# Two-layer encoder trunk on one core: the first transfers paced in the order of need, the entry's instructions kept in program order

## The chip, the core and the metric

The kernel runs on one core of one Trainium2 chip. The metric is device time in microseconds (us) for one execution, the median of repeated runs; lower is better. The engines are TensorE (PE, matmuls and transposes), VectorE (DVE), ScalarE (ACT), GpSimd (POOL) and SyncE (SP, which issues most transfers); 16 DMA engines move the data. Each engine takes its own instructions in the order in which they are listed for it and waits on semaphores for the others.

## What is computed

The reference, cut to the part that the entry of the kernel bears on (the rest of a layer in words):

```python
for l in range(DEPTH):                       # DEPTH = 2
    u = rmsnorm(x, norm_mix[l])              # x: 256 x 2048, float32
    proj = u @ w_in[l]                       # 2048 x 8256
    c_q, c_kv, k_pe, q_na, k_na, v_na, gate_a, gate_b = jnp.split(proj, IN_SPLITS, axis=-1)
    ...
    x = x + merged @ w_out[l]
    h = rmsnorm(x, norm_mlp[l]) @ w_ff1[l]   # 2048 x 8192
    x = x + jnp.square(jax.nn.relu(h)) @ w_ff2[l]
return rmsnorm(x, norm_final)
```

Between the split and `merged` stand two attentions over the 256 tokens: a latent attention (c_q, c_kv, k_pe) and a neighbourhood attention (q_na, k_na, v_na), each with 8 heads, each followed by an output projection and a sigmoid gate.

## The kernel before

**Number format.** Every matrix product is made of float32 values that are split into a high part (rounded to the format in which PE takes them) and a low part (what is left). A product is high times high, high times low and low times high, summed in PSUM. So each weight piece is first cast on ACT (`hi`, line 206) and then subtracted on DVE (`lo`, line 207), and each activation piece becomes a `pair`: the high half written by ACT, the low half by DVE (`split`, lines 164 to 171).

**Which loops run over what.** x is 256 tokens by 2048 features and stays in SBUF as two tiles `xt` (128 tokens each). For the products the features must lie on the partitions. `turned` (line 495) transposes x for two blocks of 128 features at a time: four PE transposes (line 502) into one PSUM bank, then ACT scales by the norm's gain and writes the high halves, DVE the low halves. Feature blocks in `MIXED` (pairs 1, 2, 3, that is k = 2 to 7) are first copied to a float32 tile `wide` (line 508), because a later product needs sums of them; the others go from the bank straight to a pair. The row norm itself is a sum of squares on ACT (`RowNorm.add`, line 350), one instruction for 128 tokens by 512 features; its result is only needed when the first product is read out.

The first product is the neighbourhood attention's first 512 query columns. `gemm_b` (line 277) runs over 16 blocks of k, two at a time, which makes eight steps; I call them step 0 to 7 and the weight piece of a step w0 to w7. A piece is 256 x 512 float32, 512 KB; w0 comes in two halves of 256 KB, each cast by itself. In a step PE makes 8 high matmuls (two k by four banks, line 284, 512 columns: both halves of the activation pair against the high weights) and 8 low ones (line 289, 256 columns: the high activations against the low weights). `weights` (line 181) is the generator that loads and splits the pieces; for this first product alone it loads two blocks at a time rather than four, and calls `before(k0)`, which is `enter` (line 651): it issues the loads of x that are due, makes the transposes and evictions of that step, and after every second step the norm sums of 512 features. The five small tables (mask, cos, sin and two more) are loaded at the end of it, on SP.

**What sets the order.** The program is written in one order, but the framework's scheduler sets the order within each engine by its own simulated timeline; only the bias loads of the neighbourhood heads (line 600) are kept where the program has them. Raw weight pieces have 3 buffers: a piece's transfer is issued when the low half of the third piece before it is made. `hi` and `lo` have 4 buffers each, PSUM 8 banks: the product under way holds 4 of them.

Of the kernel before, what the change touches and what calls it, by code (L numbers as in the profile page):

```python
# [39 lines left out]
P = 128  # L40
S = 256
# [34 lines left out]
def trunk(ctx: ExitStack, tc: tile.TileContext, x, w_in, w_uq, w_ukv, rpb, w_o_mla, w_o_na,  # L76
# [41 lines left out]

    def tables():
        for sb, src in ((mask_sb, mask), (cos_sb, cos), (sin_sb, sin), (turn, turns), (half, halves)):  # L120
            nc.sync.dma_start(sb, src)

    xt = [const.tile([P, D], F32, name=f"xt{t}") for t in range(2)]

# [36 lines left out]
        return acts[k]  # L161


    def split(dst, src, scale=1.0):

        nc.scalar.activation(dst[:, :S], src, AF.Copy, scale=scale)
        if isinstance(scale, float) and scale == 1.0:
            nc.vector.tensor_tensor(dst[:, S:], src, dst[:, :S].bitcast(F32), op=ALU.subtract)
        else:
            nc.vector.scalar_tensor_tensor(dst[:, S:], src, scale, dst[:, :S].bitcast(F32),  # L170
                                           op0=ALU.mult, op1=ALU.subtract)

    def parts(src):

# [6 lines left out]
    def weights(w, nk, c0, n, before=None):  # L181


        step = 2 if before else 4
        for k0 in range(0, nk, 2):
            if before:
                before(k0)
            if k0 % step == 0:
                raw = raws.tile([P, 2048], F32, tag="raw", name="raw", bufs=RBUFS)
                raw = raw[:, :step * n].rearrange("p (k n) -> p k n", n=n)  # L190
                load = w[k0 * P:(k0 + step) * P, c0:c0 + n].rearrange("(k p) n -> p k n", p=P)
                size = 1 if before and k0 == 0 else step
                for i in range(0, step, size):
                    nc.sync.dma_start(raw[:, i:i + size], load[:, i:i + size])
                if strips:
                    his, los = (t.rearrange("p (k n) -> p k n", n=n) for t in parts(raw.rearrange("p k n -> p (k n)")))
            if strips:
                yield k0, his[:, k0 % 4:k0 % 4 + 2], los[:, k0 % 4:k0 % 4 + 2]
                continue
            hi = wpool.tile([P, 1024], F32R, tag="hi", name="hi", bufs=hbufs)  # L200
            lo = wpool.tile([P, 1024], F32R, tag="lo", name="lo", bufs=hbufs)
            hi, lo = (t[:, :2 * n].rearrange("p (k n) -> p k n", n=n) for t in (hi, lo))
            src = raw[:, k0 % step:k0 % step + 2]
            for i in range(0, 2, min(size, 2)):
                i = slice(i, i + min(size, 2))
                nc.scalar.copy(hi[:, i], src[:, i])  # L206
                nc.vector.tensor_tensor(lo[:, i], src[:, i], hi[:, i].bitcast(F32), op=ALU.subtract)  # L207
            yield k0, hi, lo

    def weights_twice(w, nk, c0, n):  # L210
# [66 lines left out]
    def gemm_b(w, c0, acts, evac, before=None, ahead=None):  # L277
# [3 lines left out]
        for k0, wh, wl in weights(w, nk, c0, 512, before):  # L281
            for k in range(2):
                for m in range(4):
                    nc.tensor.matmul(ps[m], wh[:, k, m * P:(m + 1) * P], have(acts, k0 + k), start=k0 + k == 0, stop=False)  # L284
                    if m % 2:
                        tick()
            for m in range(4):
                for k in range(2):
                    nc.tensor.matmul(ps[m][:, :S], wl[:, k, m * P:(m + 1) * P], have(acts, k0 + k)[:, :S],  # L289
                                     start=False, stop=k0 + k == nk - 1)  # L290
# [51 lines left out]
    class RowNorm:  # L342
# [4 lines left out]

        def add(self, t, c4):
            junk = keep.tile([P, 512], mybir.dt.bfloat16, tag="junk", name="junk", bufs=1)
            nc.scalar.activation(junk, xt[t][:, c4 * 512:(c4 + 1) * 512], AF.Square,  # L350
                                 accum_out=self.sums[:, t, c4:c4 + 1])

        def scale(self):
            v = keep.tile([P, 2], F32, tag="var", name="var", bufs=2)
# [140 lines left out]
    def turned(src, c4, dst, scale, sums, pairs):  # L495


        for c in range(0, 4, 2):
            tp = abank()
            for i in range(2):  # L500
                for t in range(2):
                    nc.tensor.transpose(tp[:, (2 * i + t) * P:(2 * i + t + 1) * P],  # L502
                                        src(t)[:, (c + i) * P:(c + i + 1) * P], ident)
            j = 2 * c4 + c // 2
            if j in pairs:
                f = wide()
                for i in range(2):
                    nc.scalar.activation(f[:, i * S:(i + 1) * S], tp[:, i * S:(i + 1) * S], AF.Copy,
                                         scale=scale(2 * j + i))
            for i in range(2):  # L510
                a = pair()
                if j in pairs:
                    split(a, f[:, i * S:(i + 1) * S])
                else:
                    split(a, tp[:, i * S:(i + 1) * S], scale(2 * j + i))
                dst[2 * j + i] = a
            if j in pairs:
                sums[j] = f
# [125 lines left out]
    norm = RowNorm()  # L644
    xg, xf4 = [None] * NC, [None] * (NC // 2)

    def load(c0, c1):
        for t in range(2):
            nc.sync.dma_start(xt[t][:, c0:c1], x[t * P:(t + 1) * P, c0:c1])

    def enter(k0):
        if k0 in (0, 2):
# [8 lines left out]
                norm.add(t, k0 // 4)  # L661
        if k0 == 12:
            tables()

    for l in range(DEPTH):
        half_a = ExitStack()
# [298 lines left out]
```

## Time and profile before

| | us |
|---|---|
| runs before, median of 3 | 2616.18 (2616.12 to 2617.15) |
| the profiled execution's own time | 2617.45 |
| its span in the trace | 2615.3 |
| PE busy in the span | 2589.6 (99%) |
| DVE busy | 2184.0 (84%) |
| ACT busy | 1483.1 (57%) |

A profile's line gives the line of the kernel, the engine, the operation, what it writes and reads, and how often; `bank<-pair,hi` is a matmul into a PSUM bank. In a timeline the first number is the start in us from the span's beginning, the second how long the run of equal instructions took. In the chain of waits a piece ends where the next one was released. The trace of one execution is used throughout; its span is 2.15 us shorter than that execution's time.

### The profile page before, as it was taken

What the parts mean: (1) busy time and instruction counts of PE and PEld (TensorE: products, weight loads), DVE (VectorE), ACT (ScalarE), POOL (GpSimd) and SP (SyncE); (2) the same over time, 40 slices, a digit from 0 to 9 for tenths busy, and PEclk for the clock granted to TensorE, in tenths of its full rate; (3) what the DMA queues carried; (4) which work ended last, traced back from release to release, by engine and by line L of the source; (5) the groups of instructions that cost most, each with busy time, mean ns of one, the idle gap of its engine ahead of it and who ended that gap; (6) DMA issues with size and microseconds to landing.
All of it is one profiled execution on the core that took longest, in us unless ns stands there. A gap on an engine that the chain in (4) does not pass through costs nothing.

```text
span 2615.3 us, 32301 instructions
## 1 busy us (share of the span) xinstructions
PE 2589.6 (99%) x12450; PEld 2173.8 (83%) x12450; DVE 2184.0 (84%) x2571; ACT 1483.1 (57%) x1738; POOL 95.7 (4%) x117
## 2 busy tenths in 40 slices
PE   8999999999999999999999999999999999999998
PEld 7888888888888888888888888888888888888886
DVE  6678789789988898988667787896999988988885
ACT  6555556556655655556555555564666556565563
POOL 1100000000000010000001000000000000100000
PEclk9999999999999999999999999999999999999999
DMA  7555555555566575675565555544556766856753
GB/s 244 183 162 187 198 193 162 162 191 193 199 207 222 193 238 194 207 238 185 177 194 178 166 186 193 195 160 161 193 178 210 235 197 194 248 194 208 234 193 129
DMA packets 175562, 508.96 MB, mean 195 GB/s; under 512 B 13744, under 2 KB 18736, under 8 KB 175408
## 3 DMA queue, kind: packets, MB, share of 16 engines
q1 hardware_dynamic: 166496, 490.08, 56.4%
q0 software_dynamic: 8768, 16.78, 3.3%
q8 instruction: 97, 1.59, 0.2%
q14 instruction: 57, 0.47, 0.1%
q10 hardware_dynamic: 144, 0.04, 0.0%
HBM read 492.18 MB, written 2.10 MB: 189 GB/s over the span
## 4 chain that ended last, share of the span: by engine, by line
PE 88%; issue 8%; DVE 2%; ACT 1%; DMA 0%; POOL 0%; SPq 0%; POOLq 0%; DVEq 0%; ACTq 0%
PE bank L434 59%; PE bank L249 8%; PE bank L284 7%; PE bank L253 4%; PE bank L289 3%; PE bank L228 2%; PE bank L404 1%; PE bank L229 1%; PE bank L257 1%; PE bank L259 1%; PE bank L258 1%; DVE lo L178 1%; PE bank L565 1%; PE bank L502 0%; ACT hi L177 0%
## 5 line engine op out<-in xcount | busy, mean ns | idle before, releaser
L434 PE MATMUL bank<-hi,pair 128*128 128x512 f32 x5124 | 1284.4, 390 | 4.1 <-ACT hi L177 3.9
L434 PEld LDWEIGHTS bank<-hi,pair 128*128 128x128 f32 x5124 | 957.8, 188 | 204.8 <-ACT hi L177 5.6
L178 DVE TENSOR_TENSOR lo<-raw,hi 128x2048 fp32r<-128x2048 f32 (+3 forms) x416 | 741.6, 1796 | 73.8 <-ACT hi L177 47.6
L177 ACT CAST hi<-raw 128x2048 fp32r<-128x2048 f32 (+3 forms) x416 | 622.9, 1517 | 307.0 <-PE bank L434 178.6
L434 PE MATMUL bank<-lo,pair 128*128 128x512 f32 x2562 | 697.4, 390 | 0.0
L434 PEld LDWEIGHTS bank<-lo,pair 128*128 128x128 f32 x2562 | 479.7, 188 | 99.3
L177 ACT CAST hi<-sums 128x2048 fp32r<-128x2048 f32 (+1 forms) x150 | 244.9, 1637 | 291.4 <-DVE sums L475 171.8
L207 DVE TENSOR_TENSOR lo<-raw,hi 128x1024 fp32r<-128x1024 f32 (+1 forms) x225 | 273.6, 1220 | 123.0 <-ACT hi L206 121.2
L178 DVE TENSOR_TENSOR lo<-sums,hi 128x2048 fp32r<-128x2048 f32 (+1 forms) x150 | 290.8, 1947 | 98.6 <-ACT hi L177 59.0
L206 ACT CAST hi<-raw 128x1024 fp32r<-128x1024 f32 (+1 forms) x225 | 231.2, 1032 | 228.2 <-PE bank L249 88.6
L249 PE MATMUL bank<-hi,pair 128*128 128x512 f32 x1024 | 261.0, 391 | 0.0
L249 PEld LDWEIGHTS bank<-hi,pair 128*128 128x128 f32 x1024 | 190.3, 188 | 38.2
L483 DVE TENSOR_TENSOR wide<-wide,bank 128x512 f32<-128x512 f32 x336 | 214.7, 678 | 6.5 <-PE bank L434 6.4
L284 PE MATMUL bank<-pair,hi 128*128 128x512 f32 x768 | 203.3, 398 | 3.8 <-DVE pair L170 2.4
L471 DVE TENSOR_TENSOR sums<-raw 128x1024 f32<-128x1024 f32 x126 | 153.6, 1219 | 9.4 <-DMA raw<-in_w_ff 5.2
L284 PEld LDWEIGHTS bank<-pair,hi 128*128 128x128 f32 x768 | 136.3, 190 | 27.3 <-DVE pair L170 2.8
L253 PE MATMUL bank<-lo,pair 128*128 128x512 f32 x512 | 141.6, 391 | 0.0
L289 PEld LDWEIGHTS bank<-pair,lo 128*128 128x128 f32 x768 | 107.2, 191 | 8.5
L253 PEld LDWEIGHTS bank<-lo,pair 128*128 128x128 f32 x512 | 95.6, 188 | 19.4
L289 PE MATMUL bank<-pair,lo 128*128 128x256 f32 x768 | 111.7, 283 | 0.0
L413 ACT CAST pair<-wide 128x512 fp32r<-128x512 f32 x110 | 68.2, 620 | 58.6 <-DVE wide L372 56.4
L475 DVE TENSOR_TENSOR sums<-raw,sums 128x512 f32<-128x512 f32 x126 | 86.5, 687 | 2.0
(131 smaller groups left out, 1720.7 us busy)
## 6 DMA issues: line engine op xcount, KB each, us to landing
raw<-in_w_ff SPq DMA_DIRECT2D x256, 1024.0 KB, 5.2
raw<-in_w_in SPq DMA_DIRECT2D x124, 1024.0 KB, 5.0
raw<-in_w_out SPq DMA_DIRECT2D x32, 1024.0 KB, 5.3
raw<-in_w_o_na SPq DMA_DIRECT2D x16, 1024.0 KB, 5.0
raw<-in_w_o_mla SPq DMA_DIRECT2D x16, 1024.0 KB, 5.0
xt<-wide POOLq DMA_DIRECT2D x48, 256.0 KB, 5.4
raw<-in_w_ukv SPq DMA_DIRECT2D x8, 1024.0 KB, 5.0
raw<-in_w_uq SPq DMA_DIRECT2D x8, 768.0 KB, 4.5
```

Of the source, the lines that this page charges most:

```text
L177: nc.scalar.copy(hi, src)
L178: nc.vector.tensor_tensor(lo, src, hi.bitcast(F32), op=ALU.subtract)
L206: nc.scalar.copy(hi[:, i], src[:, i])
L207: nc.vector.tensor_tensor(lo[:, i], src[:, i], hi[:, i].bitcast(F32), op=ALU.subtract)
L249: nc.tensor.matmul(ps[t], a, wh[:, k], start=k0 + k + i == 0, stop=False)
L253: nc.tensor.matmul(ps[t], sides(have(acts, k0 + k), t)[0], wl[:, k], start=False, stop=k0 + k == nk - 1)
L284: nc.tensor.matmul(ps[m], wh[:, k, m * P:(m + 1) * P], have(acts, k0 + k), start=k0 + k == 0, stop=False)
L289: nc.tensor.matmul(ps[m][:, :S], wl[:, k, m * P:(m + 1) * P], have(acts, k0 + k)[:, :S], start=False, stop=k0 + k == nk - 1)
L434: nc.tensor.matmul(b[i], x, y, start=count[i] == 1, stop=count[i] == total[i])
L471: nc.vector.tensor_tensor(ts[0].rearrange("p (a n) -> p a n", a=2), raw[:, :512].rearrange("p (a n) -> p a n", a=1).to_broadcast([P, 2, 512]),
L475: final = nc.vector.tensor_tensor(t4, raw[:, 1536:], t2, op=ALU.subtract)
L483: add = lambda o, a, c: nc.vector.tensor_tensor(o, a, c, op=ALU.add)
```

## The change

Three things are changed, all of them in the entry (the first product of layer 0).

1. *Pacing.* A new function `paced` takes each load of x and of w0 to w7. It goes back over the loads before it and adds up their sizes, in units of 256 KB; the load that stands beyond three units must have landed before the new one is issued. The loads, and the tables too, are kept in program order on SP.
2. *Program order.* `pin` keeps an instruction in program order while `entering[0]` is true, up to step 7's `enter`. It is put around the high and low halves of weights and pairs, the norm sums, the copies to `wide` and the transposes, so on PE, ACT and DVE.
3. *The program's order itself.* `before(k0)` used to stand ahead of each step's weights. Now it is called for step 0 there, and for each later step in `gemm_b`, between the high and the low matmuls of the step before. Each of the two feature blocks of a step gets a PSUM bank of its own in the entry.

```diff
@@ tables()
-            nc.sync.dma_start(sb, src)
+            tc.keep_in_program_order(nc.sync.dma_start(sb, src))
...
+    entering = [True]
+    def pin(ins):
+        return tc.keep_in_program_order(ins) if entering[0] else ins
@@ weights()
         for k0 in range(0, nk, 2):
-            if before:
+            if before and k0 == 0:
                 before(k0)
...
-                    nc.sync.dma_start(raw[:, i:i + size], load[:, i:i + size])
+                    dma = nc.sync.dma_start(raw[:, i:i + size], load[:, i:i + size])
+                    if before:
+                        paced(dma, size)
...
-                nc.scalar.copy(hi[:, i], src[:, i])
-                nc.vector.tensor_tensor(lo[:, i], src[:, i], hi[:, i].bitcast(F32), op=ALU.subtract)
+                pin(nc.scalar.copy(hi[:, i], src[:, i]))
+                pin(nc.vector.tensor_tensor(lo[:, i], src[:, i], hi[:, i].bitcast(F32), op=ALU.subtract))
@@ gemm_b(), between the high and the low matmuls
+            if before and k0 + 2 < nk:
+                before(k0 + 2)
@@ turned()
-            tp = abank()
+            tp = [abank(), abank()] if entering[0] else [abank()] * 2
+            tp = [tp[i][:, i * S:(i + 1) * S] for i in range(2)]
...
+    landing = []
+    def paced(dma, tiles):
+        under_way = 0
+        for name, size in reversed(landing):
+            if under_way >= 3:
+                tc.add_manual_dep(dma.ins, name, mybir.DependencyInfo(mybir.DependencyClass.Sync,
+                                                                      mybir.DependencyReason.DATA))
+                break
+            under_way += size
+        tc.keep_in_program_order(dma)
+        landing.append((dma.ins.name, tiles))
@@ load()
-            nc.sync.dma_start(xt[t][:, c0:c1], x[t * P:(t + 1) * P, c0:c1])
+            paced(nc.sync.dma_start(xt[t][:, c0:c1], x[t * P:(t + 1) * P, c0:c1]), (c1 - c0) / 512)
@@ enter()
+        if k0 == 14:
+            entering[0] = False
```

The split, the norm sum and the transposes get `pin` in the same way. With this the lines move: 206/207 (cast and low half of weights) become 214/215, 284/289 (high and low matmuls) become 292/299, 502 (transposes) becomes 513, 508 (copy to `wide`) becomes 518, 166, 168 and 170 (pairs) become 172, 174 and 176, 350 (norm sum) becomes 360, 304 (norm's row) becomes 314, and 649 and 194 (loads of x and of weights) become 673 and 200.

What it does to the order of the instructions shows at three places. First PE, around the second step. `bank<-pair,hi` is a high matmul, `bank<-pair,lo` a low one, `bank<-ident,xt` a transpose of x for a later step; in brackets stand the semaphores that a row waits for (DMAHW0 to 7 are landings of transfers, in turn). Before, from the second four high matmuls of step 0:

```order
L284 MATMUL bank<-pair,hi 128x512 [waits DVE_49]
L284 MATMUL bank<-pair,hi 128x512 x3
L289 MATMUL bank<-pair,lo 128x256 x8
L502 MATMUL bank<-ident,xt_87 128x128 [waits DMAHW0_49]
L502 MATMUL bank<-ident,xt_87 128x128
L502 MATMUL bank<-ident,xt_88 128x128 [waits DMAHW1_49]
L502 MATMUL bank<-ident,xt_87 128x128
L502 MATMUL bank<-ident,xt_88 128x128 x2
L502 MATMUL bank<-ident,xt_87 128x128
L502 MATMUL bank<-ident,xt_88 128x128
L502 MATMUL bank<-ident,xt_87 128x128 [waits DMAHW3_49,PE_49]
L502 MATMUL bank<-ident,xt_87 128x128 [waits PE_49,Activation_49]
```

After the change, from the high matmuls of step 1:

```order
L292 MATMUL bank<-pair,hi 128x512 [waits DVE_49,Activation_49]
L292 MATMUL bank<-pair,hi 128x512 x3
L292 MATMUL bank<-pair,hi 128x512 [waits DVE_49]
L292 MATMUL bank<-pair,hi 128x512 x3
L513 MATMUL bank<-ident,xt_87 128x128 [waits DMAHW0_49,PE_49]
L513 MATMUL bank<-ident,xt_88 128x128 [waits DMAHW1_49]
L513 MATMUL bank<-ident,xt_87 128x128 [waits PE_49]
L513 MATMUL bank<-ident,xt_88 128x128
L299 MATMUL bank<-pair,lo 128x256 [waits DVE_49]
L299 MATMUL bank<-pair,lo 128x256 x7
L292 MATMUL bank<-pair,hi 128x512 [waits DVE_49,Activation_49]
```

Before, the transposes of two later steps and the beginning of a third stood together, ahead of the high matmuls of step 1. Now each step's high matmuls are followed by the transposes of the next step and then by its low matmuls, and this pattern repeats to step 6.

Second ACT, in the same stretch. `hi<-raw` is the cast of a weight piece (160 and 198 are w1 and w2 before, 162 and 201 after), `junk,sums<-xt` a norm sum, `wide<-bank` and `pair<-wide` the two instructions of an eviction. Before:

```order
L206 CAST hi_160<-raw_158 128x1024
L350 ACTIVATE junk_234,sums_89<-xt0_87 128x512
L350 ACTIVATE junk_236,sums_89<-xt1_88 128x512
L508 ACTIVATE wide_145<-bank_140,g_sb_80 128x256 x2
L166 ACTIVATE pair_148<-wide_145 128x256
L206 CAST hi_198<-raw_196 128x1024
L166 ACTIVATE pair_151<-wide_145 128x256
L350 ACTIVATE junk_306,sums_89<-xt0_87 128x512
L350 ACTIVATE junk_308,sums_89<-xt1_88 128x512
L508 ACTIVATE wide_187<-bank_182,g_sb_80 128x256 x2
L206 CAST hi_240<-raw_238 128x1024
```

After:

```order
L518 ACTIVATE wide_139<-bank_133,g_sb_80 128x256
L518 ACTIVATE wide_139<-bank_134,g_sb_80 128x256
L172 ACTIVATE pair_142<-wide_139 128x256
L172 ACTIVATE pair_145<-wide_139 128x256
L360 ACTIVATE junk_148,sums_89<-xt0_87 128x512
L360 ACTIVATE junk_150,sums_89<-xt1_88 128x512
L214 CAST hi_162<-raw_160 128x1024
L518 ACTIVATE wide_182<-bank_176,g_sb_80 128x256
L518 ACTIVATE wide_182<-bank_177,g_sb_80 128x256
L172 ACTIVATE pair_185<-wide_182 128x256
L172 ACTIVATE pair_188<-wide_182 128x256
L214 CAST hi_201<-raw_199 128x1024
```

Before, w1's cast stood ahead of the evictions of step 1 (wide_145) and w2's in the middle of them; now each cast stands behind all evictions and norm sums of its own step. The one exception is the end: behind w6's cast stand w7's and the two of the next product's first piece, and only then the evictions and norm sums of step 7. DVE has the low halves in the same new order; the reduction of the norm sums (`var`) comes after those of step 7's pairs, and one more low half of the next product's weights stands between it and the diagonals for the norm's row.

Third SP, with the loads of x (`xt<-in_x`) and of weights (`raw<-in_w_in`). Before, from the second loads of x:

```order
L649 DMA xt_87<-in_x 128x256
L649 DMA xt_88<-in_x 128x256
L194 DMA raw<-in_w_in 128x2x512
L649 DMA xt_87<-in_x 128x512 [waits DMAHW0_49]
L649 DMA xt_88<-in_x 128x512 [waits DMAHW1_49]
L194 DMA raw<-in_w_in 128x2x512 [waits DMAHW2_49]
L649 DMA xt_87<-in_x 128x512 [waits DMAHW3_49]
L649 DMA xt_88<-in_x 128x512 [waits DMAHW4_49]
L194 DMA raw<-in_w_in 128x2x512 [waits DMAHW5_49,DVE_49]
```

After:

```order
L673 DMA xt_87<-in_x 128x256
L673 DMA xt_88<-in_x 128x256 [waits DMAHW1_49]
L200 DMA raw<-in_w_in 128x2x512 [waits DMAHW2_49]
L673 DMA xt_87<-in_x 128x512 [waits DMAHW4_49,DMAHW0_49]
L673 DMA xt_88<-in_x 128x512 [waits DMAHW6_49]
L200 DMA raw<-in_w_in 128x2x512
L673 DMA xt_87<-in_x 128x512 [waits DMAHW3_49,DMAHW0_49]
L673 DMA xt_88<-in_x 128x512 [waits DMAHW1_49]
L200 DMA raw<-in_w_in 128x2x512 [waits DMAHW5_49,DVE_49]
```

The order of these nine is the same; the waits are on other landings: the second load of x for the other 128 tokens now waits for the first load of all, w1 for the second one, and so on. Further down the last loads of x stand behind w3 and w4 instead of w3 alone, and the tables behind w5 instead of ahead of w4. The table of the activation functions, which ACT loads first, now carries the wait for the gains (`g_sb`), because the first activation after it is one that uses them. After the entry the engines' orders differ again only around the output projection and the first MLP product of layer 0.

More of the change, by code (lines that the diff above doesn't have):

```diff
@@ L161, in have @@
         return acts[k]
+    entering = [True]
+    def pin(ins):
+        return tc.keep_in_program_order(ins) if entering[0] else ins
     def split(dst, src, scale=1.0):
-        nc.scalar.activation(dst[:, :S], src, AF.Copy, scale=scale)
+        pin(nc.scalar.activation(dst[:, :S], src, AF.Copy, scale=scale))
         if isinstance(scale, float) and scale == 1.0:
-            nc.vector.tensor_tensor(dst[:, S:], src, dst[:, :S].bitcast(F32), op=ALU.subtract)
+            pin(nc.vector.tensor_tensor(dst[:, S:], src, dst[:, :S].bitcast(F32), op=ALU.subtract))
         else:
-            nc.vector.scalar_tensor_tensor(dst[:, S:], src, scale, dst[:, :S].bitcast(F32),
-                                           op0=ALU.mult, op1=ALU.subtract)
+            pin(nc.vector.scalar_tensor_tensor(dst[:, S:], src, scale, dst[:, :S].bitcast(F32),
+                                               op0=ALU.mult, op1=ALU.subtract))
     def parts(src):
@@ L349, in add @@
             junk = keep.tile([P, 512], mybir.dt.bfloat16, tag="junk", name="junk", bufs=1)
-            nc.scalar.activation(junk, xt[t][:, c4 * 512:(c4 + 1) * 512], AF.Square,
-                                 accum_out=self.sums[:, t, c4:c4 + 1])
+            pin(nc.scalar.activation(junk, xt[t][:, c4 * 512:(c4 + 1) * 512], AF.Square,
+                                     accum_out=self.sums[:, t, c4:c4 + 1]))
         def scale(self):
@@ L498, in turned @@
         for c in range(0, 4, 2):
-            tp = abank()
+            tp = [abank(), abank()] if entering[0] else [abank()] * 2
+            tp = [tp[i][:, i * S:(i + 1) * S] for i in range(2)]
             for i in range(2):
                 for t in range(2):
-                    nc.tensor.transpose(tp[:, (2 * i + t) * P:(2 * i + t + 1) * P],
-                                        src(t)[:, (c + i) * P:(c + i + 1) * P], ident)
+                    pin(nc.tensor.transpose(tp[i][:, t * P:(t + 1) * P], src(t)[:, (c + i) * P:(c + i + 1) * P], ident))
             j = 2 * c4 + c // 2
@@ L507, in turned @@
                 for i in range(2):
-                    nc.scalar.activation(f[:, i * S:(i + 1) * S], tp[:, i * S:(i + 1) * S], AF.Copy,
-                                         scale=scale(2 * j + i))
+                    pin(nc.scalar.activation(f[:, i * S:(i + 1) * S], tp[i], AF.Copy,
+                                             scale=scale(2 * j + i)))
             for i in range(2):
@@ L514, in turned @@
                 else:
-                    split(a, tp[:, i * S:(i + 1) * S], scale(2 * j + i))
+                    split(a, tp[i], scale(2 * j + i))
                 dst[2 * j + i] = a
```

## The prediction

> **What bounds the kernel now.** I read the page first, then the windows of the first 30 us, then the chain of waits there, and last the waits of TensorE over the whole span. The page says who sets the time:
>
> ```profile
> PE 2589.6 (99%) x12450; PEld 2173.8 (83%) x12450; DVE 2184.0 (84%) x2571; ACT 1483.1 (57%) x1738; POOL 95.7 (4%) x117
> ```
>
> TensorE (PE) is busy 99% of the span, so a change of the entry can only move the little time in which PE stands still there. The windows (PE busy, weight loads, DVE, ACT, POOL, clock, DMA share, GB/s) show where:
>
> ```profile
> 5.00:10.00 5.00, 2.87 (x9) 2.38 (x10) 2.17 (x4) 3.10 (x8) 0.00 (x0) 1.00 0.92 255
> 10.00:15.00 5.00, 4.01 (x23) 3.41 (x21) 1.24 (x2) 3.47 (x9) 0.00 (x0) 1.00 1.01 373
> 15.00:20.00 5.00, 4.57 (x28) 3.62 (x27) 2.70 (x4) 4.97 (x12) 0.00 (x0) 1.00 0.93 283
> 20.00:25.00 5.00, 4.23 (x26) 3.58 (x25) 4.29 (x13) 5.00 (x14) 2.25 (x3) 1.00 0.55 160
> 25.00:30.00 5.00, 5.00 (x32) 4.46 (x31) 4.73 (x7) 3.41 (x7) 2.26 (x3) 1.00 0.76 223
> ```
>
> Up to 10 us PE waits for data and up to 20 us ScalarE (ACT) is full (4.97 of 5 us); from 25 us on PE is. The chain of waits (start, us, what) says the same in order of time:
>
> ```profile
> 3.54 7.94 DMA raw<-in_w_in
> ...
> 20.89 1.19 PE bank L284 x4
> ...
> 24.07 0.33 PE bank L502 x3
> 24.40 1.84 PE bank L284 x8
> 26.25 0.95 PE bank L289 x8
> ...
> 29.99 0.44 PE bank L304 x4
> ...
> 38.78 0.95 PE bank L289 x8
> ```
>
> The second weight piece, w1, lands late (7.94 us from issue), ACT then has to catch up, and from 20.89 us all is PE. A step of the first product costs PE 1.84 us for its 8 high matmuls, 0.95 for its 8 low ones, and 4 transposes at 0.11. At 38.78 + 0.95 = 39.73 us PE has done all eight steps, and beside them four high matmuls of the second product (4 x 0.23 = 0.92) and the four matmuls of the norm's row (0.44). So the first product alone ends at 39.73 - 1.36 = **38.37 us**; that is the figure to compare with.
>
> **The change, part by part.** I build the entry after the change from durations of before, in the new order of each engine. The first stretch:
>
> ```profile
> 0.74 0.40 ACTq L112 DMA_DIRECT2D g_sb<-in_gains  x1
> 1.17 1.28 ACT L206 ACT_TABLE_LOAD   x1 [1.17 <-PEq L954]
> 3.37 1.39 PE L502 MATMUL bank<-ident,xt 128*128 128x128 f32 x4 [3.37 <-DMA xt<-in_x]
> 5.34 0.62 ACT L206 CAST hi<-raw 128x512 fp32r<-128x512 f32 x1 [2.88 <-DMA raw<-in_w_in]
> 7.13 2.07 PE L284 MATMUL bank<-pair,hi 128*128 128x512 f32 x4 [2.38 <-DVE pair L170]
> 9.01 1.05 PE L502 MATMUL bank<-ident,xt 128*128 128x128 f32 x4
> 9.71 2.05 PE L284 MATMUL bank<-pair,hi 128*128 128x512 f32 x4
> g_sb<-in_gains ACTq DMA_DIRECT2D x1, 40.0 KB, 2.7
> ```
>
> The first transposes end at 3.37 + 1.39 = 4.76 as before, since the two transfers they need are still issued first. The table load now waits for the gains (issued at 0.74, landing 2.7 later, 3.44) and ends at 4.72, just in time: hidden, and 1.28 us late if those landed later. The rest of the loop's durations:
>
> ```profile
> 16.11 0.62 ACT L350 ACTIVATE junk<-xt 128x512 bf16<-128x512 f32 x1
> 17.49 0.82 ACT L508 ACTIVATE wide<-bank,g_sb 128x256 f32<-128x256 f32 x2
> 18.20 1.04 ACT L206 CAST hi<-raw 128x1024 fp32r<-128x1024 f32 x1
> 19.27 1.23 DVE L207 TENSOR_TENSOR lo<-raw,hi 128x1024 fp32r<-128x1024 f32 x1 [1.79 <-ACT hi L206]
> 21.70 0.72 ACT L166 ACTIVATE pair<-wide 128x256 fp32r<-128x256 f32 x2
> 21.92 0.27 PE L502 MATMUL bank<-ident,xt 128*128 128x128 f32 x1
> 22.32 0.47 ACT L166 ACTIVATE pair<-bank,g_sb 128x256 fp32r<-128x256 f32 x1
> 22.83 0.48 DVE L170 SCALAR_TENSOR_TENSOR pair<-bank,g_sb,pair 128x256 fp32r<-128x256 f32 x1
> 23.22 0.16 DVE L362 TENSOR_SCALAR half<-col 128x2 f32<-128x2 f32 x1
> 23.29 0.67 DVE L300 TENSOR_SCALAR diag<-ident,col 128x128 f32<-128x128 f32 x2
> 24.56 0.85 ACT L166 ACTIVATE pair<-bank,g_sb 128x256 fp32r<-128x256 f32 x2
> 25.28 1.08 ACT L206 CAST hi<-raw 128x1024 fp32r<-128x1024 f32 x1
> ```
>
> Read from start to start on ACT: two norm sums 17.49 - 16.11 = 1.38, two copies to a wide tile 0.71, two pairs from it 22.32 - 21.70 = 0.62, two pairs straight from the bank 25.28 - 24.56 = 0.72, a cast 1.04 until its user may start (19.27, 0.03 after its end).
>
> *The pinned order makes a ring.* In the new order PE has the high matmuls of step i, then the transposes of step i+1, then the low matmuls of step i, then the high ones of i+1. ACT has the evictions of step i+1, its norm sums, then the cast of w(i+1). Both take their rows in order. So the high matmuls of i+1 wait for the cast, the cast stands behind the evictions, these wait for the transposes, and those stand behind the high matmuls of step i. Only the low matmuls lie outside the ring. Before, ACT could cast a weight piece while the transposes were still to come, so it worked on during the matmuls. The ring's length, from the first high matmul of one step to that of the next: 1.84 for the high ones, two transposes issued (0.11 apart) and the second's 0.27, about 0.1 to ACT (21.92 + 0.27 = 22.19 to 22.32): 2.3. Then ACT. With wide tile and norm 2.3 + 0.71 + 0.62 + 1.38 + 1.04 + 0.05 = 6.10; with wide tile alone 4.72; from the bank with norm 5.49; from the bank alone 4.11. PE's own work in it is 1.84 + 0.43 + 0.95 = 3.22, so it stands still 0.9 to 2.9 us in each.
>
> *Start.* ACT begins at 4.8: evictions to 5.52, cast of the first half of w0 to 6.14, PE starts at 6.2 (before: 7.13). Its 8 matmuls run slowly, as the first eight of before did (four from 7.13 to 9.01, 1.88): 3.76, to 9.96; the transposes at 0.70 for four (9.01 to 9.71): two are done at 10.6, four at 10.9. ACT: copies 10.7 to 11.36, pairs to 11.98, norm to 13.36, cast to 14.4. Step 1 starts at 14.45. Whether PE is still slow there is a bound: at full rate all of it comes 3.76 - 1.84 + 0.70 - 0.43 = 2.2 earlier.
>
> *Steps 2 to 6* follow with the rings of steps 2 (wide), 3 (wide, norm), 4 (bank), 5 (bank, norm), 6 (bank): 14.45 + 4.72 + 6.10 + 4.11 + 5.49 + 4.11 = 38.98.
>
> *Step 7.* Behind the cast of w6 ACT's list has three casts (w7 and both halves of the next product's first piece, n0) ahead of the evictions of step 7. n0 may be issued when the low half of w5 is made. Transfers, in the windows at 3.5, 4.9 and 26 us, and on the page (KB each, median us to landing):
>
> ```profile
> raw<-in_w_in SPq DMA_DIRECT2D x1, 512.0 KB, 7.9
> raw<-in_w_in SPq DMA_DIRECT2D x1, 512.0 KB, 9.0
> raw<-in_w_in SPq DMA_DIRECT2D x2, 1024.0 KB, 8.4
> raw<-in_w_in SPq DMA_DIRECT2D x124, 1024.0 KB, 5.0
> ```
>
> Step 5 starts at 34.87, its cast ended 0.05 earlier, the low half of w5 at 36.08, n0 lands 5.0 later at 41.1. Casts to 43.18, first pair 43.65, DVE 0.48 more: step 7 starts at 44.2 and ends at 44.2 + 2.79 = 46.99. Then PE has the first matmul of the norm's row, which now waits: pairs to 43.90, norm sums to 45.28, a cast to 46.32, its low half on DVE to 47.58 (the column's own arithmetic lies beside it), half and the first diagonal 0.07 + 0.34. PE goes on at **48.05 us**, with the same work done as at 38.37 before.
>
> *Pacing.* w1 lands at 11.4 at the latest if pacing does nothing, and is not cast before 13.36; w2, at worst 9.0 after an issue near 7, lands at 16 for a cast at 18.1. So the earlier landings buy nothing once the ring stands, and the new waits of SP cost nothing: behind the waiting transfers on SP stand only later ones, whose users are later still. The tables now go out after w5, at about 22 us; their user on POOL feeds DVE at 85 us:
>
> ```profile
> L612 DVE SCALAR_TENSOR_TENSOR s<-bank,mb x8: 411/414/423, 85.0 to 100.0; 128x256 f32<-128x256 f32 x8
> ```
>
> *The rest.* After the entry the order differs once more, at the output projection and the first MLP product of layer 0. The largest wait of PE after the entry is 3.9 us in the whole span (who waits, for whom: us in total, times, longest), and the stretch that runs over DVE at 613 us is entered from PE, so a late PE moves it along:
>
> ```profile
> PE bank L434 <- ACT hi L177: 3.9, 4, 1.1
> ...
> 598.94 14.58 PE bank L434 x64
> ```
>
> I take 0 for it, bounds -2 and +2 (half of the 3.9, either way).
>
> **Sum.** 48.05 - 38.37 = +9.7 us. The profiled execution took 2617.45 us around a span of 2615.3; the median of the three runs is 2616.18, 1.3 lower. The difference is added to the median: **2625.9 us**. Bounds: no slow clock -2.2, n0 and the norm's chain in time -2.1 (1.1 and 1.0), later order -2: 2619.6 with all three, 2621.6 with the first two; n1, the piece behind n0, landing in 8.4 instead of 5.0 +3.4, later order +2: 2631.3.
>
> [...] The rows at 7.13 and 9.71 show PE at half speed for its first dense 4 us, while the windows grant it 1.00. [...]
>
> **Rivals.** (a) *Half rate comes back.* The longest gap, 6.10 - 3.22 = 2.9 us ahead of step 3, puts PE back to the speed of 7.13 us. A ring then grows by 1.92 + 0.27 = 2.2; two rings pass before dense work (6.4 us a step at half speed) releases it: +4.4, 2630.3. For it: slow matmuls after 2.4 us of idle at 7.13. Against: those were the first, never warm. Chance 0.13. (b) *The other side: early data wins.* The first chain link (7.94 us of w1) goes and ACT runs far enough ahead that PE is never held after 6.2. Then 3.76 + 0.70, seven steps of high ones (7 x 1.84), eight of low ones (7.6) and seven of transposes (3.1) end it at 34.2, 4.2 earlier: 2612.0, or 2609.8 with a warm clock. It decides if a cast of w(i+1) can pass the evictions; ACT's 5.00 of 5 us speaks for room on ACT being the point, the fixed rows of ACT speak against. Chance 0.08. (c) *Given back.* All 3.9 us of the later wait for casts vanish, as these get ahead of a late PE: 2622.0. Chance 0.08; against it, that stretch is entered from PE. (d) *No effect:* the rows run in another order than listed, or the ring's waits and the earlier start cancel, 2616.2. Chance 0.05; the listed order of before is the one that its trace shows.
>
> **How the numbers follow.** The ring as summed has 0.66, its time is the forecast. A measurement of this kernel tells about 0.2%, 5.2 us, from no change. Slower: the ring, (a) and (c), 0.87. Within: (d) and 0.05 of (b), 0.10. Faster: 0.03, (b) with a warm clock. The range runs from 2621 (two favourable bounds, and (c)) to 2632 (both unfavourable ones, and (a) with 1.7 us more); it leaves out (b) and (d), 0.13, and a few hundredths where several bounds meet on one side.
>
> **What would show it.** In the windows of the changed kernel PE is busy near 3.2 of every 4 to 6 us from 15 to 45 us, and ACT idles while PE runs the high matmuls. In the waits, PE's high matmuls (line 292 now) wait for the cast at line 214, five or six times, 0.9 to 2.9 us each; DMA ends no wait after 7 us. The last low matmuls of step 7 end near 47. If PE is dense from 20 us, or its waits end on pairs or DMA, the ring is wrong; matmuls of 0.43 us after 15 us show (a).

## The result, and the profile after

The changed kernel takes 2630.59 us (median of 6 executions, 2626.24 to 2631.03), the kernel before 2616.34 beside it: +14.25 us. The ratio of the mean times, here and for all runs below, is 1.0050, with a 95% interval of 1.0037 to 1.0063. The forecast was +9.7 us, 2625.9. The profiled execution took 2630.78 around a span of 2628.8.

TensorE's (PE's) rows of the timeline (start, us, ..., count, and in brackets the idle time just before and what ended it), the high matmuls of the eight steps and the first of the norm's row:

```profile
6.17 3.78 PE L292 MATMUL bank<-pair,hi 128*128 128x512 f32 x8 [1.43 <-DVE pair L176]
...
14.21 3.51 PE L292 MATMUL bank<-pair,hi 128*128 128x512 f32 x8 [2.57 <-ACT hi L214]
...
20.41 2.11 PE L292 MATMUL bank<-pair,hi 128*128 128x512 f32 x8 [1.30 <-ACT hi L214]
...
26.57 3.02 PE L292 MATMUL bank<-pair,hi 128*128 128x512 f32 x8 [2.67 <-ACT hi L214]
...
31.94 2.11 PE L292 MATMUL bank<-pair,hi 128*128 128x512 f32 x8 [0.28 <-ACT hi L214]
...
37.50 3.59 PE L292 MATMUL bank<-pair,hi 128*128 128x512 f32 x8 [2.06 <-ACT hi L214]
...
43.27 2.12 PE L292 MATMUL bank<-pair,hi 128*128 128x512 f32 x8 [0.69 <-ACT hi L214]
...
48.33 2.12 PE L292 MATMUL bank<-pair,hi 128*128 128x512 f32 x8 [1.56 <-DVE pair L176]
...
52.52 0.46 PE L314 MATMUL bank<-diag,ones 128*128 128x128 f32 x2 [1.13 <-DVE diag L310]
```

In six steps the wait ends on the cast (`ACT hi L214`), as forecast. But eight high matmuls take 2.11 us in some steps and 3.02 to 3.59 in steps 1, 3 and 5, the ones behind waits of 2.06 us or more. The norm's row starts at 52.52, against 38.37 for the same work before: +14.15, the whole loss. What lies behind it takes 2628.8 - 52.52 = 2576.3 us, before 2615.3 - 38.37 = 2576.9.

The windows of the same execution (PE, PE's weight loads, DVE, ACT, POOL, granted clock, DMA share, GB/s) show the slow steps in the clock:

```profile
5.00:10.00 5.00, 3.83 (x10) 2.95 (x11) 2.16 (x4) 1.66 (x4) 0.00 (x0) 1.00 0.86 269
10.00:15.00 5.00, 2.43 (x14) 2.13 (x13) 1.57 (x3) 3.71 (x9) 0.00 (x0) 0.89 0.84 291
15.00:20.00 5.00, 4.11 (x20) 3.28 (x18) 1.18 (x3) 2.02 (x5) 0.00 (x0) 0.77 0.69 212
20.00:25.00 5.00, 3.50 (x20) 2.90 (x20) 1.99 (x3) 2.55 (x8) 0.00 (x0) 1.00 0.44 129
25.00:30.00 5.00, 3.43 (x11) 2.69 (x12) 1.23 (x1) 1.52 (x3) 0.00 (x0) 0.75 0.37 92
```

ACT, full from 15 to 20 us before (4.97 of 5), is busy for 1.52 to 2.55 of every 5 us from 15 to 30 us here, and DMA's share there falls from 0.69 to 0.37: no engine is the bound, each waits its turn. ACT's timeline shows the ring from the other side:

```profile
25.49 1.03 ACT L214 CAST hi<-raw 128x1024 fp32r<-128x1024 f32 x1
30.05 0.90 ACT L172 ACTIVATE pair<-bank,g_sb 128x256 fp32r<-128x256 f32 x2 [3.54 <-PE bank L513]
30.85 1.04 ACT L214 CAST hi<-raw 128x1024 fp32r<-128x1024 f32 x1
```

After the cast of one piece ACT stands still for 3.54 us until PE has made the transposes (L513), not for a transfer; it evicts them at 30.05 and casts the next piece at 30.85, and PE waits for that cast.

### The profile page after: what moved, and what is told of

It is laid out like the page before. It is cut to its first block, busy times and chain, and to the rows that moved or that the text cites. A ratio compares the mean times of both kernels' runs of the same rounds, so it can differ in the third digit from the quotient of the medians.

```text
span 2628.8 us, 32302 instructions
## 1 busy us (share of the span) xinstructions
PE 2594.6 (99%) x12450; PEld 2177.0 (83%) x12450; DVE 2185.9 (83%) x2571; ACT 1482.9 (56%) x1738; POOL 98.3 (4%) x117
## 4 chain that ended last, share of the span: by engine, by line
PE 88%; issue 8%; DVE 2%; ACT 1%; DMA 1%; POOL 0%; POOLq 0%; DVEq 0%; SPq 0%; ACTq 0%
PE bank L444 59%; PE bank L257 8%; PE bank L292 7%; PE bank L261 4%; PE bank L299 3%; PE bank L236 2%; PE bank L414 1%; PE bank L237 1%; PE bank L265 1%; PE bank L267 1%; PE bank L266 1%; DVE lo L184 1%; PE bank L575 1%; PE bank L513 0%; ACT hi L214 0%
## 5 line engine op out<-in xcount | busy, mean ns | idle before, releaser
L214 ACT CAST hi<-raw 128x1024 fp32r<-128x1024 f32 (+1 forms) x225 | 230.8, 1031 | 210.8 <-PE bank L257 82.2
```

The lines of the kernel that those rows point to most:

```text
L214: pin(nc.scalar.copy(hi[:, i], src[:, i]))
```

## The experiments

Theories. **Ring**: the fixed order closes a loop cast, high matmuls, transposes, evictions, cast, and its waits are all of the loss. **Ring and clock**: those waits also bring the half clock back (0.50 granted from 13.85 to 17.26, from 27.50 to 30.92 and from 37.74 to 41.16 us), which is the 4.4 us that the ring lacks. Rivals: **transfers** (the pacing, not the order, moves the time) and **place** (the loss is at the end of the entry). In all runs the reference's work is done in full; some add idle matmuls.

**1. No pacing, order kept.**

```diff
-            if under_way >= 3:
+            if under_way >= 3 and False:
```

> The changed kernel without the pacing waits: the loads go out in the same order as soon as a buffer is free, and the listed order of PE, ACT and DVE is the changed kernel's. Theory (the ring of cast, high matmuls, transposes and evictions costs the time): w1 lands by about 11.4 us at the latest, ahead of its cast at 13.1, so nothing changes: 2628 to 2632 us, and PE's high matmuls wait for ACT's casts as in the changed kernel. Rival (the waits of the pacing hold back data that PE and ACT need): at least half of the 14 us come back, 2616 to 2623.

Measured: 2629.24 us (2626.78 to 2631.81), ratio to before 1.0051 (1.0038 to 1.0063). The loss stays, so the pacing isn't its cause. Two rows of PE:

```profile
13.69 2.12 PE L292 MATMUL bank<-pair,hi 128*128 128x512 f32 x8 [2.67 <-ACT hi L214]
...
24.67 2.51 PE L292 MATMUL bank<-pair,hi 128*128 128x512 f32 x8 [2.67 <-ACT hi L214]
```

The same waits for casts. Here one wait of 2.67 us is followed by full speed. Behind the next, just as long, the matmuls begin at full speed too, and the granted clock falls to 0.50 only at 26.20 us, for 3.41 us; the step's eight low matmuls then take 2.06 instead of 1.20. In this trace the clock does not follow the length of a wait alone.

**2. Pacing alone, on the kernel before** (and the five tables keep their place on SP).

```diff
-            nc.sync.dma_start(xt[t][:, c0:c1], x[t * P:(t + 1) * P, c0:c1])
+            paced(nc.sync.dma_start(xt[t][:, c0:c1], x[t * P:(t + 1) * P, c0:c1]), (c1 - c0) / 512)
...
+                    if before:
+                        paced(dma, size)
```

> The kernel before with the pacing alone: the loads and the tables in program order with the pacing waits, no instruction of PE, ACT or DVE pinned, the transposes called ahead of each step's weights as before. Theory (ring): no ring, so no loss; w1 lands by 8 to 9 us instead of 11.48, which is worth 0 to 3 us: 2613 to 2617. Rival (pacing holds data back): 2624 to 2631.

Measured: 2617.36 (2615.79 to 2619.88), ratio 1.0005 (0.9996 to 1.0014): no difference that can be told, 0.4 above the expected range. PE's waits in its first 55 us:

```profile
PE bank L504 <- DMA xt<-in_x: 6.3, 4, 3.3
```

Beside the first 3.3 us, which the kernel before has too, PE waits another 3.0 us for x in three pieces, the longest 1.66. Step 1 starts earlier (14.11 rather than 15.47), and the later x takes that back.

**3. No fixed order, pacing kept.**

```diff
     def pin(ins):
-        return tc.keep_in_program_order(ins) if entering[0] else ins
+        return ins
```

> The changed kernel without the pins on PE, ACT and DVE (pacing, the moved call of the transposes and the two banks stay), so the scheduler sets these orders: it lists w1's cast ahead of step 1's evictions. Theory (ring): the ring is open, PE is dense from about 20 us on as before: 2612 to 2618. Rival (pacing, or the new place of the transposes, not the pinned order): 2626 to 2631.

Measured: 2619.78 (2617.68 to 2621.92), ratio 1.0013 (1.0005 to 1.0022). Of the loss of 14.25 us 4.0 are left, so some 10 go with the fixed order, but the time is 1.8 above the upper end I gave. The rows of PE, then of ACT, show where:

```profile
31.70 0.60 PE L314 MATMUL bank<-diag,ones 128*128 128x128 f32 x4
34.98 1.51 PE L292 MATMUL bank<-pair,hi 128*128 128x512 f32 x4 [2.67 <-DVE pair L176]
36.28 1.91 PE L299 MATMUL bank<-pair,lo 128*128 128x256 f32 x8
```

```profile
30.33 1.99 ACT L214 CAST hi<-raw 128x1024 fp32r<-128x1024 f32 x2 [2.93 <-DMA raw<-in_w_in]
32.23 1.20 ACT L172 ACTIVATE pair<-bank,g_sb 128x256 fp32r<-128x256 f32 x3
```

PE is dense from 20 to 31 us, then the second half of step 6 waits 2.67 us for its eviction. The scheduler put this and step 7's two evictions behind the next product's first casts, which themselves waited 2.93 us for their transfer; the granted clock is down after it (0.66 from 35 to 40 us, and 1.91 for eight low matmuls that take 1.11 to 1.20 elsewhere). So there is a second place, the end of the entry.

**4. The ring opened by one position.** The cast of the next weight piece stands ahead of the evictions of the next step, all else fixed as it was:

```diff
             if before and k0 + 2 < nk:
-                before(k0 + 2)
+                before.fetch(k0 + 2)
+                piece = next(pieces)
+                before(k0 + 2)
```

> The changed kernel with everything pinned and paced as it is, but each next weight piece is fetched and cast ahead of the evictions of its step, so ACT's list is cast of w(i+1), evictions of step i+1, norm sums. Theory (ring): the ring loses the cast (1.04) and the norm sums (1.38 in every second step); what is left, high matmuls, transposes, one copy or none, one pair and its low half, is 3.3 to 3.8 us a step against PE's own 3.2, with no gap over 1 us up to step 6, so the half clock does not come back: step 7 starts near 33 us instead of 48.3 and the time is 2612 to 2617. Rival (pinning as such, or pacing, costs the time): 2626 to 2631.

Measured: 2617.82 (2616.49 to 2621.5), ratio 1.0010 (1.0001 to 1.0019); 0.8 above the range. Of its timeline, steps 5 to 7 and the norm's row:

```profile
30.77 2.11 PE L296 MATMUL bank<-pair,hi 128*128 128x512 f32 x8 [0.30 <-DVE pair L176]
...
36.43 3.55 PE L296 MATMUL bank<-pair,hi 128*128 128x512 f32 x8 [2.16 <-DVE pair L176]
...
40.89 0.38 PE L321 MATMUL bank<-diag,ones 128*128 128x128 f32 x2
```

From step 1 to step 6 the steps start 3.4 to 4.0 us apart, near PE's own work, with waits of at most 0.53: one move, of the cast with its low half, opens the ring and takes 12.2 of the 14.25 us. The rest is step 7, whose evictions stand behind three casts and three low halves, and the half clock after 2.16 us of waiting (0.67 granted from 35 to 40 us; eight high matmuls in 3.55).

**5. The norm sums out of the ring** (behind the cast of their step instead of ahead of it; the end of the pinned stretch moves with the last of them):

```diff
         for k0, wh, wl in weights(w, nk, c0, 512, before):
+            if before:
+                before.sums(k0)
```

> The changed kernel with only the norm sums moved: they stand behind the cast of their step instead of ahead of it, so that they run on ACT while PE has the high matmuls. Theory (ring, with the half clock brought on by its gaps): the rings of steps 1, 3 and 5 shorten by 1.38 each, 4.1 in all, and with the gaps of 2.1 to 2.7 us cut to 0.7 to 1.3 the half clock stays away and another 0 to 4.4 come back: 2622 to 2627, the rings of steps 3 and 5 at 4.7 and 4.1 us. Rival (ACT's order does not matter, PE is held by something else): 2629 to 2632.

Measured: 2627.58 (2626.88 to 2628.25), 0.6 above the range. The two rings with sums shrink from 6.16 and 5.56 to 4.80 and 4.19, by about the 1.38 us of the sums, no wait in them exceeds 1.31 us, the clock stays at 1.00, and step 7 starts at 39.31, 9.0 earlier than in the changed kernel. Then:

```profile
39.31 2.14 PE L294 MATMUL bank<-pair,hi 128*128 128x512 f32 x8 [0.69 <-ACT hi L214]
...
47.32 0.77 PE L316 MATMUL bank<-diag,ones 128*128 128x128 f32 x2 [4.93 <-DVE diag L312]
...
47.74 3.76 PE L294 MATMUL bank<-pair,hi 128*128 128x512 f32 x8
```

The norm's diagonal is 4.93 us late, and the clock falls in that wait (0.57 granted from 45 to 50 us and 0.74 from 50 to 55; eight high matmuls in 3.76). The last norm sum now stands behind two of the next product's casts (it starts at 41.66), and on DVE two more low halves and three read-outs of the product stand between the reduction of the sums (43.13) and the diagonal (46.77). Most of the gain is given back at the next place in the same chain.

**6. The waits filled, to keep the clock up.** Idle matmuls of a 128x128 tile of ones behind the low halves of steps 0, 2 and 4:

```diff
+            if before and k0 in (0, 4, 8):
+                idle = abank()
+                for i in range(16):
+                    pin(nc.tensor.matmul(idle[:, :P], ones, ident, start=True, stop=True))
```

> The changed kernel with 16 matmuls of 128 columns, whose result is not used, behind the low matmuls of steps 0, 2 and 4, that is inside PE's three gaps of 2.1 to 2.7 us (16 x 0.11 = 1.8 us of work in each). Theory (the half clock is brought on by these gaps): the windows from 12 to 45 us show a granted clock of 1.00, the eight high matmuls of steps 1, 3 and 5 start to end take 2.1 us instead of 3.0 to 3.6, and the time falls by about 4 us to 2626 or 2627. Rival (the clock falls for another reason, or its cost is hidden): no change or slower by the work added, 2630 to 2634.

Measured: 2630.4 (2629.7 to 2632.44). The price was wrong: each of these matmuls shows as two instructions of PE, so 16 took

```profile
12.09 3.73 PE L304 MATMUL bank<-ident,ones 128*128 128x128 f32 x32
15.58 2.08 PE L292 MATMUL bank<-pair,hi 128*128 128x512 f32 x8
```

3.73 us instead of the 1.8 meant, and made the three rings 0.7 to 1.4 us longer. The eight high matmuls of steps 1, 3 and 5 did run at full speed (2.08 to 2.10 us, 1.00 granted up to 45 us). The test says that the clock stayed up behind the three filled waits, and nothing yet of what that is worth.

**7. The same with 8 instead of 16**, so that the filler ends inside the wait.

> As the changed kernel, with 8 idle 128x128 matmuls of ones (16 instructions of TensorE, 1.75 us by the 3.73 us that 32 took in the run with 16) behind the low halves of steps 0, 2 and 4, in the waits of 2.57, 2.67 and 2.06 us after which the changed kernel ran at half clock. Nothing of the reference's work is left out. If the half clock is what the ring of the forecast lacked: the filler no longer outlasts the waits, eight high matmuls take 2.1 us in steps 1, 3 and 5, and the time is 2626 to 2627.5. If the ring alone is longer than was worked out and the clock only follows it: 2629.5 to 2631, though the matmuls are fast.

Measured: 2626.62 (2626.54 to 2626.92), ratio 1.0041 (1.0028 to 1.0053). The rows of steps 1, 3 and 5, with the filler ahead of the first, and of step 7 and the norm's row:

```profile
11.05 1.95 PE L304 MATMUL bank<-ident,ones 128*128 128x128 f32 x16
13.88 2.13 PE L292 MATMUL bank<-pair,hi 128*128 128x512 f32 x8 [0.89 <-ACT hi L214]
...
24.87 2.13 PE L292 MATMUL bank<-pair,hi 128*128 128x512 f32 x8 [0.88 <-ACT hi L214]
...
34.64 2.12 PE L292 MATMUL bank<-pair,hi 128*128 128x512 f32 x8 [0.27 <-ACT hi L214]
...
44.95 2.11 PE L292 MATMUL bank<-pair,hi 128*128 128x512 f32 x8 [2.61 <-DVE pair L176]
...
48.12 0.46 PE L318 MATMUL bank<-diag,ones 128*128 128x128 f32 x2
```

Work that computes nothing makes the kernel 4.0 us faster: the half clock was real, and what remains is the ring as it was summed: from the start of step 1 to that of step 6 the rings measure 4.83, 6.16, 4.22, 5.55 and 4.20 against 4.72, 6.10, 4.11, 5.49 and 4.11. That the norm's row starts at 48.12 where the forecast had 48.05 is in part luck: step 1 starts 0.57 earlier, step 7 comes 0.89 later behind step 6, and the row then has no wait where 1.06 was forecast. All five executions lie within 0.4 us at a mean clock of 0.999. The changed kernel's spread over 5 us, with its one execution of 2626.24 at 0.999 and the others at 0.995 to 0.997, fits a clock that falls in some executions and not in others.

**8. Run 4, with the next product's first casts and low halves behind step 7's evictions and sums.**

```diff
+                    if held[0]:
+                        held[0] -= 1
+                        for ins in last.values():
...
+                                behind.enter_context(tc.issue_after(ins))
```

> The cast of the next piece stands ahead of the evictions, as in the run that opened the ring, and the next product's first two casts and low halves stand behind step 7's evictions and norm sums on ScalarE and VectorE. Nothing of the computation is left out. If step 7's wait of 2.16 us and the half clock behind it were all that was left: step 7 starts 2 to 2.5 earlier than 36.43 and its eight matmuls take 2.1 rather than 3.55, so the time is about 3 below the 2617.8 of that run: 2614 to 2616, a tie with the kernel before or up to 2 under it. If those casts are needed where they stood (the next product then waits for its weights): 2617 to 2619.

Measured: 2616.52 (2616.2 to 2616.81), ratio 1.0001 (0.9992 to 1.0010): a tie with the kernel before, 0.5 above the range.

```profile
34.20 2.12 PE L305 MATMUL bank<-pair,hi 128*128 128x512 f32 x8
...
37.97 0.46 PE L330 MATMUL bank<-diag,ones 128*128 128x128 f32 x2 [0.70 <-DVE diag L326]
```

Step 7 starts 2.23 us earlier than in run 4, at full speed. The end of the entry was the second place, and two moves have undone the whole loss.

**9. Run 8, with the transposes two steps ahead of their use.**

```diff
+                if k0 + 4 < nk:
+                    before.fetch(k0 + 4)
+                    if k0:
+                        before(k0 + 4)
```

> As the run with the next product's casts behind step 7, and the transposes stand two steps ahead of their use instead of one, the third step's behind the first low halves. Nothing of the computation is left out. If the ring is the whole cost of the order: the evictions have a step of TensorE's work to hide behind, no wait over 1 us is left on TensorE from step 2 on, and the time is 2612 to 2615, below the kernel before by 1 to 4. If dense matmuls are held by something else (transfers of x, which are now needed a step sooner): a wait of 1 to 3 us for x in steps 1 to 3, and 2615 to 2618.

Measured: 2613.52 (2612.98 to 2613.68), ratio 0.9990 (0.9981 to 0.9999). From step 4 on PE's rows follow each other without a wait:

```profile
22.21 2.00 PE L305 MATMUL bank<-pair,hi 128*128 128x512 f32 x8
24.06 0.60 PE L539 MATMUL bank<-ident,xt 128*128 128x128 f32 x4
24.41 1.19 PE L322 MATMUL bank<-pair,lo 128*128 128x256 f32 x8
25.44 2.00 PE L305 MATMUL bank<-pair,hi 128*128 128x512 f32 x8
...
34.26 0.38 PE L340 MATMUL bank<-diag,ones 128*128 128x128 f32 x2
```

A step takes 3.23 us, PE's own 3.22 of the prediction. The norm's row starts at 34.26; the prediction's rival (b), PE never held after 6.2, put it at 34.2.

**10. Run 9, warmed.** Five idle matmuls of ones ahead of the first transposes and three behind them:

```diff
+                for i in range(5):
+                    pin(nc.tensor.matmul(idle[:, :P], ones, ones, start=True, stop=True))
                 before(k0)
+                for i in range(3):
+                    pin(nc.tensor.matmul(idle[:, :P], ones, ones, start=True, stop=True))
```

> As the run two steps ahead, and 5 idle matmuls of ones stand ahead of the first transposes and 3 behind them, in TensorE's first wait. Nothing of the computation is left out. In the changed kernel the first step's matmuls ran at half clock (4 took about 2 us). If the clock at the start is worth something: the first step's matmuls are done up to 2 us sooner and the time is 0 to 2 below the run two steps ahead. If the second step then waits for its data (the second piece's cast ends at 12.6 to 13.1): no difference within 0.6.

Measured: 2611.76 (2611.29 to 2613.56), ratio 0.9984 (0.9975 to 0.9993): 1.8 below run 9, 4.4 below the kernel before, and the best of all versions.

```profile
4.64 1.49 PE L202 MATMUL bank<-ones 128*128 128x128 f32 x6
6.15 2.12 PE L310 MATMUL bank<-pair,hi 128*128 128x512 f32 x8
...
33.79 0.38 PE L345 MATMUL bank<-diag,ones 128*128 128x128 f32 x2
```

The first step's eight take 2.12 us instead of 3.6. Then PE waits 1.15 for x, so the norm's row gains only 0.47; between the two profiled spans lie 1.1 us, of which the other 0.6 comes after it and is not explained.

**11. Run 10 without pacing** (the edit of run 1).

> As the warmed run two steps ahead, but the transfers don't wait for those two or three behind: no pacing, the order of the queue kept. Nothing of the computation is left out. If pacing is worth nothing (the forecast's claim, so far seen with the ring closed and on the kernel before): 2611.2 to 2612.4, the same as the warmed run's 2611.8. If pacing helps where TensorE waits for nothing else, because the pieces under way no longer share the engines with the later ones: x lands later in steps 0 and 1, the wait for x of 1.15 us grows to 2 to 3, and the time is 2613 to 2615.

Measured: 2613.94 (2612.0 to 2617.09), ratio 0.9993 (0.9983 to 1.0002). Ten of the eleven executions lie at 2612.5 or above, where ten of run 10's eleven lie at 2612.09 or below: with the ring open, pacing is probably worth about 2 us and a smaller spread, though the two intervals overlap. Not by the wait I named: its one trace has 0.36 us of waiting for x, less than run 10, and 0.78 for a pair in step 1. That trace is of the fast end of the spread (2612.5), so where the others lose stays open.

**12. The kernel before, warmed** as in run 10.

> The kernel before, with the same 5 and 3 idle matmuls of ones ahead of and behind its first transposes, and nothing else. If the warmed run owes its last 1.8 us to the first step's clock alone, the same is to be had here: the first eight high matmuls take 2.1 us in all rather than 4.1, and the time is 0.5 to 2 below before: 2614 to 2615.7. If what follows waits for data (before's step 1 began at 15.47, after a wait for x of 0.99 and one for evictions): 2615.8 to 2616.5, no difference.

Measured: 2613.28 (2611.87 to 2614.17), ratio 0.9988 (0.9979 to 0.9997), more than I expected. It is not the clean test that I meant. The first four matmuls still take 2.07 us, and without a fixed order the eight added matmuls made the scheduler deal the entry out anew: the first four high matmuls of step 1 now stand ahead of the last two transposes, for which the kernel before waited 0.99 us. Step 0 ends 0.74 us earlier than before (its low matmuls at 12.23 instead of 12.97), though it starts no earlier (7.18, 7.13): its last four high matmuls take 1.52 us instead of 2.05, its low ones 1.12 instead of 1.41, so that much is clock. How the rest divides, this run does not tell.

## Why the prediction was right in kind and short in size

- *The ring*: right. Starts forecast 14.45, 19.17, 25.27, 29.38, 34.87, 38.98, 44.2; measured 14.21, 20.41, 26.57, 31.94, 37.50, 43.27, 48.33. From start to start, rings 2, 4 and 6 (behind the slow steps 1, 3 and 5) measure 6.20, 5.37 and 5.77 against 4.72, 4.11 and 4.11: 1.48, 1.26 and 1.66 over, 4.40 together. Rings 3 and 5 measure 6.16 and 5.56 against 6.10 and 5.49. The reading that ACT is full up to 20 us before was loose (3.47 of 5 us from 10 to 15, and still 5.00 from 20 to 25), but no term of the ring rests on it.
- *The clock*: the step that failed is in the sum, which took full speed for all steps behind the first, and in the price given to rival (a). I let the half clock return only in the longest gap, 2.9 us ahead of step 3, with a chance of 0.13. It returned behind 2.57, 2.67 and 2.06 us. The size, +4.4, came out as that rival had it, but by luck: by three steps of about 1.5 and not by two of 2.2. With run 7 the two parts stand apart: about 4 us of clock, about 10 of ring.
- *Full speed behind a wait*: that every wait of the ring, up to 2.9 us, leaves PE at full speed was my assumption, and no run shows it. Of ten waits of 1.80 to 2.67 us on PE behind the first step, in the changed kernel and runs 1, 3, 4 and 7, eight were followed by slow matmuls. The other two are one of 2.67 in run 1 and the one of 2.61 in run 7; how the first of them lay stands in the last section.
- *Step 7 and the norm's row*: sized right (5.06 against 5.22; a stall of 1.13 against 1.06), but for a different reason, so that the sizes agree is luck. I had the evictions held by ACT's three casts; the wait ended on DVE, whose four low halves stand ahead of step 7's pairs, and the row itself waited for a transfer, seen in DVE's timeline and in the chain of waits:

```profile
43.24 4.63 DVE L215 TENSOR_TENSOR lo<-raw,hi 128x1024 fp32r<-128x1024 f32 x4 [0.42 <-ACT hi L214]
47.79 0.87 DVE L176 SCALAR_TENSOR_TENSOR pair<-bank,g_sb,pair 128x256 fp32r<-128x256 f32 x2
```

```profile
44.50 5.23 DMA raw<-in_w_in
49.81 1.06 ACT hi L214
50.89 0.57 DVE lo L215
```

  "DMA ends no wait after 7 us" is true of PE and missed this one of ACT, 1.65 us for n1, which the prediction had only as a bound.
- *Pacing*: right under its condition. "Buys nothing once the ring stands" is run 1; on the kernel before it is run 2; with the ring open it is probably worth about 2 us (run 11).
- *The later order*: 0 forecast, -0.6 between the two traces; the wait of 3.9 us at the later line is there unchanged:

```profile
PE bank L444 <- ACT hi L183: 3.9, 4, 1.1
```

- *The other rivals*: (b) did not come, but its end point did when the order was mended (34.26 and 33.79 against 34.2). (c) and (d) did not occur.

## What to carry over

Before fixing the order of several in-order engines, write one turn of the loop as a chain from engine to engine and add it up: here one cast behind instead of ahead of the evictions made a chain of 4 to 6 us out of steps that cost TensorE 3.2, and moving that cast with its low half took back 12 of 14 us. Look at the end of the fixed stretch too, where the next loop's work queues ahead of the last step. And price a wait on TensorE at more than its length, since the matmuls behind it may run slower: here they did behind eight of ten waits of 1.80 to 2.67 us, and filling three of them took off 4.0 us.

## What the runs showed of the hardware that was not expected

- The half clock came back after waits as short as 1.80 us (run 1, step 7: eight high matmuls in 2.77 us instead of 2.1, 0.67 granted from 45 to 50 us) and stayed away after others of 2.61 (run 7, 2.11 us) and 2.67 (run 1, step 1, 2.12 us). In the first 55 us of the fourteen traces the granted clock falls ten times in all, each time in or behind a wait of PE of 1.80 to 4.93 us, and behind the first step no wait of 1.66 us or less was followed by slow matmuls. So in these traces the length alone does not decide. Narrower windows show how the two waits of 2.67 us lay in run 1 (stretch and its length, PE's busy time and instructions, granted clock, DMA share, GB/s):

```profile
9.13:12.55 3.42, 1.90 (x14) 1.00 1.00 343
12.55:15.96 3.41, 2.27 (x11) 1.00 0.45 173
22.79:26.20 3.41, 1.53 (x7) 1.00 0.38 107
26.20:29.61 3.41, 3.41 (x16) 0.50 0.55 154
```

  The first of these waits was shared by two stretches (1.52 and 1.14 us idle), and the clock stayed at 1.00; of the second, 1.88 us fell into one, and in the next the clock was at 0.50. In the changed kernel it is at 0.50 from 13.85 to 17.26, from 27.50 to 30.92 and from 37.74 to 41.16 us, 3.41 us each time, and these starts lie four and three times 3.41 apart. In the 3.41 us ahead of each of the three, PE is idle for 2.21, 2.48 and 2.06 us. In steps of 3.41 us from 10.44 us, where that trace's clock record begins, it is idle for 1.30 us at most in every other stretch at 1.00 up to 58 us. The fall in run 1, at 26.20 us, lies 4.6 such steps behind 10.44, so the same steps do not fit both traces. That the same kernel's times scatter (2626.24 to 2631.03) because such steps lie differently in each execution is my guess, and not tested.
- The half clock shows in the granted clock when it comes back (0.75 to 0.91 in the windows of 5 us of the changed kernel), but not at the start: the first step's eight matmuls take 3.78 us in a window with 1.00. The clock record has no entry before 10.44 us there, and the eight low matmuls that start at 10.44 take 1.20.
- With 16 idle 128x128 instructions, 8 matmuls, in the first 6 us, the first step's eight took 2.12 us in run 10. In run 12 the same were not enough: after the last of them PE waited 1.26 us, and the first four high matmuls took 2.07, the next four 1.52 and the eight low ones 1.12.
- A 128x128 matmul of 32-bit ones showed as two instructions of about 0.12 us each at a granted clock of 1.00 (run 6: 16 matmuls, 32 instructions, 3.73 us).
